# Two added waits in the start of a planned kernel: weight copies behind the first staging tile, and squares from the sixth token tile on

## The chip, the cores and the metric

The kernel runs on one core of a Trainium2 chip. Its metric is device time in microseconds (us) for one execution, as the median of several runs; lower is better. TensorE (PE) multiplies matrices, ScalarE (ACT), VectorE (DVE) and GpSimd (POOL) work element by element, and SyncE (SP) issues all of this kernel's DMAs from one queue, in program order. Each engine executes its own instructions in program order and waits on semaphores for the results of others.

## The reference, cut to what matters

One layer of a generator over 1024 latent tokens and 256 context tokens of width 1024, in float32. Both token sets are normalised, modulated and projected; two branches (gated linear attention and differential attention) follow, are merged and projected back. The change touches only the first two lines:

```python
def rms_norm(t):
    tf = t.astype(jnp.float32)
    return (tf * lax.rsqrt(jnp.mean(tf * tf, axis=-1, keepdims=True) + EPS)).astype(t.dtype)

mod_x = jax.nn.silu(c) @ w_ada[layer] + b_ada[layer]       # shift, scale, gate: 3 x 1024
mod_c = jax.nn.silu(c_ctx) @ w_ada[layer] + b_ada[layer]
h  = rms_norm(x) * (1 + sc_x) + sh_x                        # (1024, 1024)
hc = rms_norm(ctx) * (1 + sc_c) + sh_c                      # (256, 1024)
pl, pc = h @ w_in, hc @ w_in                                # eleven projections, 9248 columns
...
x = x + g_x * (y @ w_out)                                   # after both branches
```

## The kernel before, in words

**How the order comes about.** The program is written by a planner (`Driver`). Every piece of work is a Python generator that yields times, events or buffers; the planner keeps a clock of its own with a cost for each instruction, wakes the generators in the order of due time and priority (a lower number goes first), and the instructions are emitted in the order in which the generators run. The order on PE, ACT, DVE, POOL and in SP's queue is thus fixed when the program is built. An event such as `ev_h[k, half]` is set at the planned end of the work that it stands for; a generator that yields it resumes from then on. `acq(tag)` takes one of the buffers of a tag and waits until one is free. A few pieces have planned dates: the low-rank preparation 60 us, the output gate 70 us, late constants 105 us.

**Precision.** A float32 operand of a large product is split into a high part (fp32r) and a low part (the difference); a product is three matrix products (`mm3`, all emitted at line 349, high x high, high x low, low x high). Weights are split by an ACT copy for the high part and a DVE subtraction for the low part (`split`).

**The start of the program** (`prologue`, line 505, and `wstream`, line 686):

- *Token tiles.* Ten tiles of 128 tokens: 0 to 7 are latent, 8 and 9 context. `xnorm(i)` (line 515) takes a scratch buffer `p`, squares the tile on ACT with a sum (1024 elements per partition), forms the inverse root on POOL (two small instructions) and scales the tile on DVE. Tiles 0 to 3 are loaded early, between pieces of `w_ada`; tiles 4 to 9 after the modulation weights have been converted. Six tile buffers (`g5`) exist.
- *Modulation.* `w_ada` comes in two halves of the channels. The first half is used in float32 from tag `w` (`ada(0)`); the second is staged in tags `l5` and `raw` in turn, by 128 rows (row blocks 0 to 7), and split into tags `w` (even row blocks) and `pl` (odd ones; it holds the pieces of just one row block) by `conv` (line 566, priority -2), then multiplied on PE into `gs` and `go` (`ada(1)`). Each half ends in a small tile of shifts and scales, `shsc`.
- *Modulated channel blocks.* For each half of the latent tokens and then the context, and for each channel block k of 128 channels, PE transposes the normalised tiles into one of two `tp` buffers (line 375), and `hblock(k, half)` (line 640) modulates them on ACT (`p<-tp,shsc`), rounds the high part on POOL (`h<-p`) and subtracts on DVE (`h<-p,h`). Then `ev_h[k, half]` is set. Blocks 0 to 3 need the first half of `shsc`, blocks 4 to 7 the second. After block 7 the tile buffers of that half come free.
- *Projection weights.* `wstream` loads `w_in` into `raw` staging tiles of 256 rows (two blocks of 128), three buffers shared with the odd row blocks of `w_ada`, and splits them into tag `w` (18 buffers) with priority 3. The first stream has gates: its first two staging tiles are loaded behind the first half of `w_ada` (`RAWS = 2`), the others behind the second half; the splitting of the third and later ones waits until `conv` has ended. The split of the first two waits only for their data. A staging buffer comes free when both of its blocks have been split.
- *The first projection job.* `job_tr` (line 806) multiplies block by block: a first group of three outputs of 128 x 512, row blocks 0 to 7 with nine matrix products each (72), for the first half of the tokens, then a fourth group (24 products), then the context and the second half. It has priority 9, `ada` -1.

After the start, PE works through the projections, then both branches and the output.

The few lines around the change, in `wstream.run`:

```python
            for x, (n, src, c0, kk) in enumerate(queue):
                yield loaded[x]
                if gate and x == self.RAWS:
                    yield gate[2]
```

Of the kernel before, what the change touches and what calls it, by code (L numbers as in the profile page):

```python
# [232 lines left out]
class Hybrid:  # L233
# [271 lines left out]
    def prologue(self):  # L505
# [7 lines left out]
            self.dma(xs[i], a["x"][0, i * P:(i + 1) * P] if i < 8 else a["ctx"][0, (i - 8) * P:(i - 7) * P])  # L513

        def xnorm(i):
            yield from self.acq("p")
            sq = self.t("p", [P, D], BF16)
            ss = self.t("sm", [P, 1])
            yield self.d.when(xs[i])
            self.rel("p", self.act.activation(sq, xs[i], AF.Square, accum_out=ss))  # L520
            yield self.d.when(ss)
            self.pool.tensor_scalar(ss, ss, 1.0 / D, EPS, ALU.mult, ALU.add)
            yield self.pool.tensor_tensor(ss, ss, self.nhalf[:, 0:1], ALU.pow)
            self.d.set(ev_x[i], self.dve.tensor_scalar(xs[i], xs[i], ss, None, ALU.mult))
# [7 lines left out]
        def loads():  # L532

            for part in range(2):
                for k in range(NK):
                    src = wada[k * P:(k + 1) * P, 0:2048].rearrange("p (s h c) -> p s h c", h=2, c=512)[:, :, part]
                    ev = ev_w[k, part]
                    if part == 0:
                        yield from self.acq("w", 2)
                        ev.w = [self.t("w", [P, 512]) for _ in range(2)]  # L540
                        for s in range(2):
                            self.dma(ev.w[s], src[:, s])
                        d.set(ev, d.when(*ev.w))
                    else:
                        tg = ("l5", "raw")[k % 2]
                        yield from self.acq(tg)
                        raw = self.t(tg, [P, 2, 512])
                        self.dma(raw, src)
                        ev_r[k].raw = tg, raw
                        d.set(ev_r[k], d.when(raw))  # L550
                    for i in self.XL[part].get(k, ()):
                        yield from self.acq("g5")
                        xload(i)
                        self.d.spawn(xnorm(i))
                if part == 0:
                    d.set(self.ev_wl[0])
                    for x in range(self.RAWS):
                        yield self.wload[x]
            d.set(self.ev_wl[1])
            yield self.ev_wc  # L560
            for i in range(4, 10):
                yield from self.acq("g5")
                xload(i)
                self.d.spawn(xnorm(i))
# [121 lines left out]
    def wstream(self, jobs, tag, gate=None, prio=3, after=()):  # L686

        queue = [(n, src, c0, kk) for n, (src, c0) in enumerate(jobs) for kk in range(NK // 2)]
        wd = Weights({(n, k): Event() for n in range(len(jobs)) for k in range(NK)})
        loaded = [Event() for _ in queue]  # L690

        def load():
            for ev in after[:1]:
                yield ev
            for x, (n, src, c0, kk) in enumerate(queue):
                if gate and x in (0, self.RAWS):
                    yield gate[x > 0]
                yield from self.acq("raw")
                raw = self.t("raw", [P, 2, 512])
                loaded[x].raw = raw  # L700
                self.d.set(loaded[x], self.dma(raw, src[kk * 256:(kk + 1) * 256, c0:c0 + 512].rearrange(
                    "(k p) c -> p k c", p=P)))

        def run():
            for ev in after[1:]:
                yield ev
            for x, (n, src, c0, kk) in enumerate(queue):
                yield loaded[x]
                if gate and x == self.RAWS:
                    yield gate[2]  # L710
                raw = loaded[x].raw
                for j in range(2):
                    yield from self.acq(tag, 2)
                    hi = self.t(tag, [P, 512], F32R)
                    lo = self.t(tag, [P, 512], F32R)
                    e = yield from self.split(raw[:, j], hi, lo)
                    ev = wd[n, 2 * kk + j]
                    ev.w = (hi, lo)
                    self.d.set(ev, e)
                self.rel("raw", e)  # L720

        self.d.spawn(load(), prio=prio)
        self.d.spawn(run(), prio=prio)
        wd.loaded = loaded
        return wd
# [2080 lines left out]
```

## Time and profile before

| What | Value |
|---|---|
| median of 3 runs | 1617.54 us (1617.53 to 1622.0) |
| profiled execution, own time | 1616.59 us |
| its span | 1614.9 us, 24351 instructions |
| PE busy | 1590.6 us, 98% of the span |
| PE busy in the first 60 us | 48.67 us |
| DVE, ACT, POOL busy | 76%, 52%, 39% |
| HBM | 204 GB/s over the span |
| granted TensorE clock | 1.00 |

The times in the rows of the trace are from the span's start: the start, then the duration, the engine, the line, the operation, the output and inputs by tile names, the shapes, and the number of merged instructions; in brackets how long the engine stood idle before it and what ended that. Line 201 is the helper through which all ACT, DVE and POOL instructions go, 314 all DMAs, so one goes by tile names: `w<-raw` is a split of projection weights, `w<-l` and `pl<-raw` splits of modulation weights, `p<-g` the square of a token tile, `g<-g,sm` its scaling. Durations of PE rows are modelled and overlap, so the pace is read from starts.

### The profile page before, as it was taken

Reading aid. Unit: us, or ns where it says so; the run is one execution under the profiler, and the core shown is the slowest. Engines: PE = TensorE matmul, PEld = TensorE weight load, DVE = VectorE, ACT = ScalarE, POOL = GpSimd, SP = SyncE. Lnnn points to the kernel's source line nnn. Section 1 sums busy time; section 2 is a strip of 40 time slices with the busy share of each in tenths; the row PEclk is TensorE's granted clock in tenths of the full one; section 3 lists DMA queues with packets and bytes.
Section 4 is the critical chain, followed back from the end, with each engine's and each line's share of the span. In section 5 each row is a group of like instructions: output and inputs, shape, how many; then the busy total and the mean of one; then the engine's idle time right before and its main releaser. Section 6 shows DMA issues by size and latency. Waiting matters only on the chain.

```text
span 1614.9 us, 24351 instructions
## 1 busy us (share of the span) xinstructions
PE 1590.6 (98%) x8229; PEld 1328.0 (82%) x8229; DVE 1223.5 (76%) x2117; ACT 836.2 (52%) x1719; POOL 634.2 (39%) x663
## 2 busy tenths in 40 slices
PE   7999999999999999999999999999999999999999
PEld 3788888888888888888888788888888888888887
DVE  4787945576877779767677688878788888889994
ACT  4776523445343454655435466665665656656331
POOL 1500000001325667535464256656765666560000
PEclk9999999999999999999999999999999999999999
DMA  8576896998778467564645944545587555348662
GB/s 310 199 256 242 330 305 230 343 328 297 275 246 267 123 198 233 163 212 122 185 118 165 251 116 121 151 128 150 151 265 218 158 136 151 112 152 280 210 206 100
DMA packets 259565, 331.16 MB, mean 205 GB/s; under 512 B 22600, under 2 KB 160752, under 8 KB 259440
## 3 DMA queue, kind: packets, MB, share of 16 engines
q1 hardware_dynamic: 259440, 329.60, 63.7%
q8 instruction: 65, 1.06, 0.3%
q14 instruction: 60, 0.49, 0.1%
HBM read 225.20 MB, written 104.33 MB: 204 GB/s over the span
## 4 chain that ended last, share of the span: by engine, by line
PE 91%; DVE 4%; ACT 1%; DMA 1%; POOL 1%; issue 1%; SPq 0%; ACTq 0%; DVEq 0%; POOLq 0%
PE mm L349 31%; PE mb L349 11%; PE s L349 8%; PE mc L349 7%; PE b L349 6%; PE tp L349 6%; PE gt L349 5%; PE b L375 4%; PE gs L349 4%; PE go L349 4%; PE mz L349 2%; PE tp L375 2%; DVE sm L201 1%; POOL at L201 1%; DMA w<-in_w_ada 1%
## 5 line engine op out<-in xcount | busy, mean ns | idle before, releaser
L349 PE MATMUL mm<-w,h 128*128 128x512 f32 x912 | 231.0, 400 | 0.0
L349 PE MATMUL mb<-h,wt 128*128 128x512 f32 x840 | 222.8, 400 | 0.0
L201 DVE TENSOR_REDUCE sm<-s 128x1 f32<-128x1024 f32 (+1 forms) x192 | 193.3, 1037 | 16.4 <-PE s L349 9.9
L201 ACT ACTIVATE e<-s,sm 128x1280 f32<-128x1280 f32 x128 | 169.3, 1328 | 57.7 <-DVE sm L201 54.5
L349 PEld LDWEIGHTS mm<-w,h 128*128 128x128 f32 x912 | 167.4, 188 | 32.7
L201 POOL TENSOR_TENSOR at<-ac,at 128x512 fp32r<-128x512 f32 x128 | 186.6, 1458 | 10.7
L349 PEld LDWEIGHTS mb<-h,wt 128*128 128x128 f32 x840 | 151.4, 188 | 28.7 <-DVE ft L201 0.3
L201 POOL TENSOR_SCALAR at<-ac 128x512 fp32r<-128x512 f32 x128 | 98.4, 768 | 192.2 <-ACT ac L201 191.7
L349 PE MATMUL s<-hk,aq 128*128 128x512 f32 x744 | 169.2, 364 | 1.9 <-ACT e L201 1.8
L349 PE MATMUL mm<-h,w 128*128 128x512 f32 x672 | 168.2, 400 | 1.1 <-DVE h L201 1.1
L349 PEld LDWEIGHTS mm<-h,w 128*128 128x128 f32 x672 | 123.7, 188 | 26.5 <-DVE h L201 1.6
L201 DVE TENSOR_TENSOR w<-raw,w 128x512 fp32r<-128x512 f32 x128 | 95.7, 764 | 53.4 <-ACT w L201 51.2
L349 PEld LDWEIGHTS s<-hk,aq 128*128 128x128 f32 x744 | 117.6, 189 | 19.1 <-ACT e L201 4.3
L349 PE MATMUL b<-at,vv 128*128 128x256 f32 x960 | 130.1, 287 | 1.1 <-ACT ac L201 0.8
L349 PEld LDWEIGHTS b<-at,vv 128*128 128x128 f32 x960 | 119.5, 191 | 2.8 <-ACT ac L201 1.0
L201 ACT ACTIVATE w<-raw 128x512 fp32r<-128x512 f32 x128 | 78.1, 626 | 84.0 <-PE tp L349 23.8
L201 DVE SCALAR_TENSOR_TENSOR e<-e,sm,e 128x1280 f32<-128x1280 f32 x64 | 118.3, 1849 | 0.9
L201 ACT ACTIVATE ac<-b 128x512 f32<-128x512 f32 x122 | 72.4, 598 | 88.8 <-PE b L375 87.1
L201 POOL TENSOR_TENSOR sm<-sm,nhalf 128x2 f32<-128x2 f32 (+2 forms) x94 | 107.2, 1141 | 28.1 <-DVE sm L201 22.8
L349 PE MATMUL mm<-w,g 128*128 128x512 f32 x432 | 105.7, 389 | 0.0
L349 PEld LDWEIGHTS mm<-w,g 128*128 128x128 f32 x432 | 81.1, 188 | 16.8
L375 PE MATMUL b<-ident,e 128*128 128x128 f32 x610 | 92.6, 273 | 1.3 <-ACT ac L201 0.8
(353 smaller groups left out, 3050.8 us busy)
## 6 DMA issues: line engine op xcount, KB each, us to landing
raw<-in_w_in SPq DMA_DIRECT2D x62, 512.0 KB, 4.2
g<-d_s SPq DMA_DIRECT2D x32, 640.0 KB, 6.3
g<-d_s SPq DMA_DIRECT2D x32, 512.0 KB, 5.8
aq<-d_qT SPq DMA_DIRECT2D x124, 128.0 KB, 3.3
d_dv<-pl SPq DMA_DIRECT2D x40, 256.0 KB, 3.3
gv<-d_v SPq DMA_DIRECT2D x40, 256.0 KB, 3.2
d_kT<-pl SPq DMA_DIRECT2D x40, 256.0 KB, 2.7
hk<-d_kT SPq DMA_DIRECT2D x32, 320.0 KB, 5.7
```

The lines of the kernel that those rows point to most:

```text
L201: self.ins = f(out, *args, **kw).ins
L349: self.ins = self.nc.tensor.matmul(out, lhsT, rhs, start=start, stop=stop, skip_group_check=more).ins
L375: self.nc.tensor.transpose(out, src, self.ident[:n, :n])
```

## The change

Two waits are added. A normalisation `xnorm(i)` of tile 5 and later does not take its scratch buffer, and so does not square its tile, before channel block 5 of the first half of the tokens has been finished (`ev_h[5, 0]`). And in the first weight stream, which alone has gates, the split of the second staging tile (x == 1, projection rows 256 to 511) does not begin before channel block 1 of the first half has been finished (`ev_h[1, 0]`). No instruction is added or removed; loads are written by the same generators as before.

```diff
         def xnorm(i):
+            if i >= 5:
+                yield self.ev_h[5, 0]
             yield from self.acq("p")
             sq = self.t("p", [P, D], BF16)
             ss = self.t("sm", [P, 1])
...
                 yield loaded[x]
                 if gate and x == self.RAWS:
                     yield gate[2]
+                if gate and x == 1:
+                    yield self.ev_h[1, 0]
                 raw = loaded[x].raw
                 for j in range(2):
                     yield from self.acq(tag, 2)
```

## The prediction

> **What bounds the kernel now.** I read the page first (engines, slices), then busy time by stage, then the instructions in order of time on each engine between 22 and 62 us.
>
> ```profile
> span 1614.9 us, 24351 instructions
> PE 1590.6 (98%) x8229; PEld 1328.0 (82%) x8229; DVE 1223.5 (76%) x2117; ACT 836.2 (52%) x1719; POOL 634.2 (39%) x663
> ```
>
> ```profile
> 24.00:28.00 4.00, 2.89 (x22) 2.22 (x22) 3.30 (x8) 3.66 (x7) 1.40 (x2) 1.00 1.05 379
> 28.00:32.00 4.00, 4.00 (x19) 3.20 (x19) 3.59 (x5) 3.85 (x8) 1.98 (x3) 1.00 0.88 328
> 32.00:36.00 4.00, 4.00 (x17) 1.35 (x16) 4.00 (x8) 2.29 (x4) 0.00 (x0) 1.00 0.59 187
> ...
> 44.00:50.60 6.60, 3.82 (x28) 2.59 (x26) 5.34 (x11) 6.52 (x12) 4.02 (x7) 1.00 0.88 273
> 60.00:500.00 440.00, 438.68 (x2004) 363.55 (x2003) 308.41 (x462) 211.01 (x344) 57.97 (x55) 1.00 0.78 274
> 500.00:900.00 400.00, 398.48 (x2003) 335.34 (x2002) 293.28 (x551) 192.78 (x514) 216.37 (x269) 1.00 0.60 178
> 900.00:1614.90 714.90, 704.80 (x4031) 604.90 (x4030) 588.97 (x1050) 397.29 (x801) 343.17 (x304) 1.00 0.56 169
> ```
>
> The columns of a stage are its length, then busy time of PE, PEld, DVE, ACT and POOL, the granted clock, DMA share and GB/s. After 60 us PE is idle for only 1.32 + 1.52 + 10.10 = 12.9 us in 1555 us, so PE work sets the end there, and the granted clock is 1.00 in every stage shown. The change can act where PE is not yet fed: 24 to 28 us (1.11 us idle) and 44 to 50.6 us (2.78 us idle). Both holes are the same event: PE has transposed the first token tiles and waits until the channel blocks have been modulated (ACT), rounded to the high part (POOL) and given their low part (DVE).
>
> **Holding back the second staging tile.** The first hole, engine by engine:
>
> ```profile
> 24.65 1.15 ACT L201 ACTIVATE w<-raw 128x512 fp32r<-128x512 f32 x2 [0.21 <-DMA raw<-in_w_in]
> 25.71 3.02 ACT L201 ACTIVATE p<-tp,shsc 128x512 f32<-128x512 f32 x4
> ```
>
> ```profile
> 24.41 1.09 PE L375 MATMUL tp<-ident,g 128*128 128x128 f32 x8
> ...
> 27.60 4.50 PE L349 MATMUL mm<-h,w 128*128 128x512 f32 x18
> ...
> 35.25 2.92 PE L349 MATMUL mm<-h,w 128*128 128x512 f32 x12
> 38.01 0.63 PE L349 MATMUL gs<-pl,cs 128*2 128x512 f32 x2
> ```
>
> ```profile
> 24.72 1.89 DVE L201 TENSOR_TENSOR w<-raw,w 128x512 fp32r<-128x512 f32 x3
> 27.21 0.69 DVE L201 TENSOR_TENSOR h<-p,h 128x512 fp32r<-128x512 f32 x1 [0.60 <-POOL h L201]
> 28.41 2.11 DVE L201 TENSOR_TENSOR h<-p,h 128x512 fp32r<-128x512 f32 x2 [0.51 <-POOL h L201]
> ...
> 34.66 1.28 DVE L201 TENSOR_TENSOR pl<-raw,pl 128x512 fp32r<-128x512 f32 x2
> ```
>
> The ACT pair at 24.65 is what the new wait moves. It ends at 25.80 and the first modulation follows it directly. Its own input is there earlier: four of the eight transposes of 1.09 us are done at about 24.95. With about 0.1 us of handover (an estimate, the size of the small gaps between these rows) it could start at 25.05. *Gain: 25.71 - 25.05 = 0.66 us*, and the chain behind it (POOL, DVE, the 18 products at 27.60) moves along.
>
> What is moved comes back: two ACT copies (1.15 us) and two DVE subtractions (two thirds of 1.89, 1.26 us), now behind channel block 1's subtraction, which ends at 29.46 here and at 28.8 then. There ACT is busy for 3.85 of 4 us and DVE for 3.59 and 4.00 of 4, so on those engines nothing hides them: what follows on DVE, the pieces of the second half of the modulation weights, comes up to 1.26 - 0.66 = 0.60 us later than now. On PE it is hidden. PE has 18 products (4.50 us) before it needs block 2 of the projection weights, and the third pair of modulation pieces (DVE 34.66 + 1.28 = 35.94) is not used on PE before 38.01: 2.07 us of cover. I take 0. The bounds are +0.60, and -2.07 if PE's written order now takes that piece as soon as it is there.
>
> The third thing is a buffer. There are three staging buffers, and the load behind the second tile goes through the one SP queue:
>
> ```profile
> 26.64 0.37 SPq L314 DMA_DIRECT2D raw<-in_w_ada  x1
> ```
>
> ```profile
> raw<-in_w_ada SPq DMA_DIRECT2D x4, 512.0 KB, 5.9
> ```
>
> ```profile
> 38.44 1.15 ACT L201 ACTIVATE pl<-raw 128x512 fp32r<-128x512 f32 x2 [2.75 <-PE gs L349]
> ```
>
> The load at 26.64 (modulation row block 5) leaves when the second tile's subtractions end. They would end at 28.8 + 0.6 (first copy) + 1.3 (two subtractions) = 30.7 at the earliest, and 2.5 us later, 33.2, if row blocks 0 and 1 are copied first (four subtractions). With 5.9 us to land, block 5 is there at 36.6 to 39.1. It is copied at 38.44 now, which is 37.8 after the gain. I take 0; the upper bound is 39.1 - 37.8 = 1.3 us. What stands behind it in SP's order is held with it.
>
> **Holding back the squares.** The second hole:
>
> ```profile
> 46.01 1.04 ACT L201 ACTIVATE p<-g 128x1024 bf16<-128x1024 f32 x1
> 46.96 0.19 ACT L201 ACTIVATION_READ_ACCUMULATOR p<-g 128x1 f32 x1
> 47.05 1.43 ACT L201 ACTIVATE p<-tp,shsc 128x512 f32<-128x512 f32 x2
> ```
>
> ```profile
> 46.20 0.17 DVE L201 TENSOR_TENSOR shsc<-shsc,gt 128x16 f32<-128x16 f32 x1
> ...
> 48.36 1.10 DVE L201 TENSOR_SCALAR g<-g,sm 128x1024 f32<-128x1024 f32 x1 [0.72 <-POOL sm L201]
> 49.39 1.08 DVE L201 TENSOR_TENSOR h<-p,h 128x512 fp32r<-128x512 f32 x1
> ```
>
> ```profile
> 47.77 0.56 POOL L201 TENSOR_TENSOR sm<-sm,nhalf 128x1 f32<-128x1 f32 x1
> 48.30 3.67 POOL L201 TENSOR_SCALAR h<-p 128x512 fp32r<-128x512 f32 x4
> ```
>
> ```profile
> 50.53 8.25 PE L349 MATMUL mm<-h,w 128*128 128x512 f32 x35 [1.05 <-DVE h L201]
> 58.62 1.03 PE L375 MATMUL tp<-ident,g 128*128 128x128 f32 x8
> ```
>
> Tile 5 is in the way of channel block 4 three times. On ACT its square delays the modulation from about 46.45 (shift and scale end at 46.37) to 47.05: 0.60 us. On POOL its power ends at 48.33, and block 4's rounding starts at 48.30 instead of about 47.3 (the modulation would end near 47.2): 1.0 us. On DVE its scaling ends at 49.46, and block 4's subtraction starts at 49.39; without both it would start where the rounding ends, 47.3 + 0.92 + 0.15 = 48.4 (0.92 is a quarter of 3.67, 0.15 an estimated handover): again 1.0 us. PE waits for that subtraction at 50.53. These are one path, so *the gain is 1.0 us*, not the sum. Lower bound 0.45, if a weight copy of 0.58 us (half of 1.15) takes the slot on ACT: the modulation then still starts near 47.05, but POOL takes it up at its end, near 47.85, instead of at 48.30; upper bound 1.4, if the subtraction, no longer entangled with the scaling, takes 0.69 instead of 1.08.
>
> The 1.08 us stands beside a busy POOL; the same shape takes 0.69 at 27.21. [...]
>
> Where does tile 5 go? Behind block 5's subtraction, into these gaps:
>
> ```profile
> 53.07 1.06 ACT L201 ACTIVATE p<-g 128x1024 bf16<-128x1024 f32 x1 [2.21 <-DMA g<-in_x]
> ```
>
> ```profile
> 54.31 0.19 POOL L201 TENSOR_SCALAR sm<-sm 128x1 f32<-128x1 f32 x1 [2.34 <-ACT p L201]
> ```
>
> ```profile
> 55.16 0.75 DVE L201 TENSOR_SCALAR g<-g,sm 128x1024 f32<-128x1024 f32 x1 [0.85 <-POOL sm L201]
> 56.64 0.75 DVE L201 TENSOR_SCALAR g<-g,sm 128x1024 f32<-128x1024 f32 x1 [0.72 <-POOL sm L201]
> ```
>
> ACT has 2.21 us for the square and the read of its sum (1.04 + 0.19), POOL 2.34 for 0.19 + 0.56, DVE 0.85 for 0.75: cost 0. Tiles 6 to 9 get the same wait, but their data lands only at 53.07, after block 5's subtraction (about 52.5). If the gaps were gone, tile 7's scaling (end 57.39) would come up to 1.23 us later, just at its use on PE at 58.62, which itself moves to 57.0; bounds 0 to +1.6 (57.39 + 1.23 - 57.0).
>
> **After the holes.** A gain in front is kept only if PE has other work until the second half of the tokens is modulated. One job has a fixed date: the low-rank preparation starts at a planned 60 us.
>
> ```profile
> 59.41 3.66 PE L349 MATMUL mm<-h,w 128*128 128x512 f32 x15
> ...
> 63.26 1.63 PE L349 MATMUL mm<-h,pl 128*128 128x512 f32 x6
> ```
>
> The fourth group has 24 products, 15 of them here, so 9 x 0.24 us (3.66 / 15) = 2.2 us are left to fill in front of the low-rank work. That covers 1.66 us.
>
> **Sum.** -0.66 + 0 + 0 - 1.0 + 0 = -1.66 us. The profiled execution took 1616.59 us (its span and 1.69 us around it), so 1614.9 us for that one; it stands 0.95 us below the median of the runs, and against the median of 1617.54 the sum gives 1615.9 us. About 0.3%, 4.85 us, is what a measurement can tell from no change; the sum is a third of it.
>
> **The rivals.**
>
> *The held copies come too late* (slower). Place: row block 5 of the modulation weights, behind the second staging buffer on SP. For it: in 28 to 36 us ACT and DVE are full, and the planner gives the modulation copies priority over the projection copies. If row blocks 0 to 2 go first, the second tile is done at 34.66 (where the third pair starts) - 0.66 + 1.26 = 35.3, block 5 lands at 41.2 instead of being copied at 37.8, and the chain behind it is 3.4 us late: -1.66 + 3.4 = +1.8, or 1619.3 us. The point from which it decides: release at 37.8 - 5.9 = 31.9 starts to cost, and from 33.6 on the whole is slower than before. Against it: the wait opens at 28.8, about when the four modulations end on ACT and the copies of row block 0 can start (25.71 + 3.02 = 28.73 now).
>
> *The modulation chain closes up* (faster). PE now writes 12 products (35.25) ahead of the third pair, which is ready 2.07 us earlier. With block 2's weights later the planner may put the pair first: -1.66 - 2.07 = -3.7, or 1613.8 us. Against it: the products then have to fill later gaps.
>
> *Hidden anyway.* The freed ACT slots go to weight copies (0.58 us each): the first gain is eaten by the 0.60 us on DVE, of the second 0.45 us is left. That is about -0.4 us, between 0 and -0.9, or 1617.1 us.
>
> *The rest is written anew.* The order on every engine comes from a planner whose clock starts earlier, while 60, 70 and 105 us stay fixed dates. The 12.9 us of PE idle after 60 us could shrink or grow by a third to a half, 4 to 6 us: about 1611 or 1623 us. For it: the stretch from 900 us, where 10.1 of the 12.9 us lie. Against it: the dates bear on work of the first 120 us, and from 60 to 500 us PE is idle for only 1.32 us.
>
> **How the numbers follow.** Chances: my forecast (a gain of 0.9 to 2.7 us) 0.38; hidden anyway 0.17; held copies late 0.13; chain closes up 0.10; order written anew, faster 0.10 and slower 0.12. The first four lie within 0.3%: 0.78; faster 0.10, slower 0.12. The likeliest case's own range is 1614.8 to 1616.7 us. The range takes the first four (1613.8 to 1619.3, with their bounds about 1613 to 1621) and about half of either tail of the last: 1611.5 to 1622.0.
>
> **What would show it.** First modulation (ACT, now 25.71) at about 25.05 with the copy pair behind the four modulations; block 4's subtraction on DVE near 48.4 - 0.7 = 47.7, and PE's long run of products, now from 50.53, from about 48.9; no scaling of tile 5 before it, its square near 50 to 52; the transposes at 58.62 near 57.0. Wrong would be: the load of row block 5 leaving after 32 us; its copy waiting for the DMA rather than for PE; DVE idle in front of tile 7's scaling; or PE idle after 60 us other than 12.9 us, by 2 us or more, which would mean that the later order moved and not the start.

## The result and the profile after

The changed kernel takes 1621.18 us (median; 1618.52 to 1624.29), the kernel before in the same series 1618.73 us (1617.08 to 1622.26). The ratio is 1.0014, with an interval of 1.0008 to 1.0021: **slower by about 2.4 us**. That is less than the 0.3% which the prediction counted as no change, and inside its range. But the interval excludes the forecast gain of 1.66 us (0.999).

Two cautions on single profiles. The profiled execution of before (1616.59 us) lies below all 19 executions timed here. That of after (1623.29 us) is the second longest of its kernel's 19. A second profile of after (1621.22 us) sits at its median, and the accounting below uses that one. The profiled executions also begin up to 1.0 us apart, so milestones are counted from the first copy of projection weights on ACT (23.30 us in before, 24.03 in after, 23.54 in the second profile of after, 24.30 with the squares alone held and the constants late).

The page of after, and its busy time by stage (length, then busy time of PE, PEld, DVE, ACT and POOL, the granted clock, DMA share and GB/s):

```profile
span 1621.5 us, 24358 instructions
PE 1593.9 (98%) x8229; PEld 1329.0 (82%) x8229; DVE 1224.5 (76%) x2117; ACT 836.3 (52%) x1719; POOL 633.9 (39%) x663
```

```profile
40.00:44.00 4.00, 2.70 (x12) 0.88 (x10) 2.00 (x4) 2.66 (x6) 0.00 (x0) 1.00 0.76 295
44.00:50.60 6.60, 5.35 (x30) 2.93 (x31) 5.55 (x12) 5.73 (x11) 1.84 (x4) 0.92 0.91 310
50.60:60.00 9.40, 9.40 (x40) 7.84 (x40) 5.98 (x8) 6.17 (x10) 4.42 (x9) 0.88 1.00 346
60.00:500.00 440.00, 435.40 (x1987) 359.42 (x1986) 304.68 (x457) 211.45 (x347) 57.48 (x57) 1.00 0.77 271
```

Two stages are new against before: PE is idle for 1.30 us between 40 and 44 us, and for 4.60 us instead of 1.32 between 60 and 500 us. The clock below 1.00 is treated at the end.

ACT of after in order of time:

```profile
24.03 1.15 ACT L201 ACTIVATE w<-raw 128x512 fp32r<-128x512 f32 x2 [0.37 <-DMA raw<-in_w_in]
25.89 3.04 ACT L201 ACTIVATE p<-tp,shsc 128x512 f32<-128x512 f32 x4 [0.71 <-PE tp L375]
...
29.86 0.62 ACT L201 ACTIVATE w<-raw 128x512 fp32r<-128x512 f32 x1
...
31.43 0.62 ACT L201 ACTIVATE w<-raw 128x512 fp32r<-128x512 f32 x1
...
41.34 1.15 ACT L201 ACTIVATE pl<-raw 128x512 fp32r<-128x512 f32 x2 [4.60 <-DMA raw<-in_w_ada]
...
69.44 0.78 ACT L201 ACTIVATE p<-tp,shsc 128x512 f32<-128x512 f32 x1 [3.44 <-DMA d_k<-p]
```

The first row is the first staging tile; the first modulation follows it without the second tile between. The two held copies come at 29.86 and 31.43, one by one, between copies of modulation weights. Then two waits for a DMA: 4.60 us for row block 5 of the modulation weights, and 3.44 us for a *store* (`d_k<-p`). The store matters because it holds a scratch buffer `p` that the next modulation needs.

DVE and SP of after show why row block 5 is late:

```profile
33.06 0.68 DVE L201 TENSOR_TENSOR w<-raw,w 128x512 fp32r<-128x512 f32 x1
33.66 0.68 DVE L201 TENSOR_TENSOR pl<-raw,pl 128x512 fp32r<-128x512 f32 x1
34.26 0.68 DVE L201 TENSOR_TENSOR w<-raw,w 128x512 fp32r<-128x512 f32 x1
```

```profile
32.56 0.37 SPq L314 DMA_DIRECT2D l<-in_w_ada  x1
34.37 0.97 SPq L314 DMA_DIRECT2D raw<-in_w_ada  x2
...
50.82 0.82 SPq L314 DMA_DIRECT2D g<-in_x  x2
...
55.18 3.07 SPq L314 DMA_DIRECT2D gains<-in_diff_q_norm  x1
...
62.12 3.09 SPq L314 DMA_DIRECT2D d_k<-p  x3
```

The held tile's second subtraction ends at 34.94, and only then is its staging buffer free. With it held, the loads of row blocks 5 and 7 leave SP as a pair, one at 34.37 and one at 34.97, behind the load of row block 6 (32.56). The first of the pair is row block 5. By the times it takes the buffer of row block 1, whose second subtraction (33.66) ends at 34.34; the held tile's own buffer goes to row block 7. In before, row block 5 took the second staging tile's buffer and left at 26.64; row block 7 left at 33.55. The later rows show the second new thing. The loads of constants (`gains` and three like it) stand right ahead of the stores, and SP is held 3.07 us at the first of them. In before three of the four stood ahead of the token tiles and only `gdif` behind them, and three stores took 1.32 us to issue:

```profile
45.29 0.46 SPq L314 DMA_DIRECT2D gains<-in_diff_q_norm  x1
...
48.89 0.81 SPq L314 DMA_DIRECT2D g<-in_x  x2
...
52.46 1.83 SPq L314 DMA_DIRECT2D gdif<-in_diff_norm  x1
...
58.56 1.32 SPq L314 DMA_DIRECT2D d_k<-p  x3
```

From issue to landing the same three stores take 3.1 us in before and 7.3 in after (5.6 in its second profile):

```profile
d_k<-p SPq DMA_DIRECT2D x3, 256.0 KB, 3.1
```

```profile
d_k<-p SPq DMA_DIRECT2D x3, 256.0 KB, 7.3
```

While the stores stand behind the constants, little moves. In the second profile of after, where SP issues them from 60.92 on and they land after 68 us, the DMA share (the last figure but one) is 0.19 and 0.22 before it rises again:

```profile
60.00:62.00 2.00, 1.39 (x8) 0.97 (x6) 1.05 (x2) 2.00 (x7) 1.28 (x3) 1.00 0.19 52
62.00:64.00 2.00, 2.00 (x10) 1.64 (x9) 1.00 (x4) 2.00 (x9) 0.00 (x0) 1.00 0.22 80
64.00:66.00 2.00, 2.00 (x13) 1.58 (x12) 1.55 (x2) 0.80 (x2) 1.75 (x2) 1.00 0.88 321
```

PE of after shows what each costs:

```profile
42.75 0.62 PE L349 MATMUL gs<-pl,cs 128*2 128x512 f32 x2 [1.30 <-DVE pl L201]
...
51.08 9.30 PE L349 MATMUL mm<-h,w 128*128 128x512 f32 x36
...
60.98 0.77 PE L375 MATMUL tp<-ident,g 128*128 128x128 f32 x5 [0.26 <-DVE g L201]
62.15 3.71 PE L349 MATMUL mm<-h,w 128*128 128x512 f32 x15 [0.41 <-ACT p L201]
...
70.27 0.66 PE L375 MATMUL tp<-ident,g 128*128 128x128 f32 x4 [2.16 <-ACT p L201]
```

**Milestones in us behind the first weight copy.** Each is read from the start of a row on ACT or PE, less that of the copy; "last modulation product" is the last product of the second half of `w_ada`, "first use of block 4's low part" the 38th projection product. The long wait of PE behind the stores (70.27 above) stands before later transposes of the second half than the milestone, which is the first of them. The second profile of before took 1619.20 us.

| | before | before, 2nd profile | after, 2nd profile | squares only, constants late | both, row block 5 elsewhere, constants late |
|---|---|---|---|---|---|
| first modulation (ACT) | 2.41 | 2.40 | 1.86 | 2.41 | 1.87 |
| last modulation product | 20.62 | 21.18 | 21.90 | 20.61 | 19.95 |
| first use of block 4's low part | 27.23 | 28.60 | 27.28 | 26.22 | 26.22 |
| second half's first transposes | 35.32 | 37.45 | 35.36 | 34.31 | 34.66 |
| seventh low-rank product | 42.22 | 44.36 | 46.30 | 41.97 | 41.18 |
| first product `mm<-hk,w` | 55.39 | 57.53 | 59.48 | 55.14 | 58.43 |
| end | 1591.56 | 1593.70 | 1595.85 | 1592.60 | 1598.88 |

In the second profile of after, up to the second half's first transposes everything cancels against the first profile of before (+0.04 us): row block 5 costs 1.28, and block 4 gives 1.23 back. Between there and the seventh low-rank product 4.04 us are lost, and behind 75 us little more: +4.09 at the first product `mm<-hk,w`, +4.29 at the end.

The medians differ by only 2.4 us, and the second profile of before shows a reason. It has lost 2.13 us by the second half's first transposes, and nothing behind them. Its clock was at half for 3.41 us twice (the last section), and one weight copy waited for its data just ahead of block 4:

```profile
47.47 0.63 ACT L201 ACTIVATE w<-raw 128x512 fp32r<-128x512 f32 x1 [1.05 <-DMA raw<-in_w_in]
```

Against that profile after loses 2.15 us (1595.85 - 1593.70). The runs' mean granted clocks say the same. Of 86 executions of before in the experiments' series, 22 have a mean clock of 1.000, with a median of 1617.69 us. Of the 30 executions of after on record it is 15, with a median of 1621.18. Without loss of clock the change thus costs about 3.5 us. The medians of all executions show less, since before lost clock in more of its executions; why it did is not shown.

### The profile page after: what moved, and what is told of

The parts are those of the page before. It is cut to its first block, busy times and chain, and to the rows that moved or that the text cites. A ratio compares the mean times of both kernels' runs of the same rounds, so it can differ in the third digit from the quotient of the medians.

```text
span 1621.5 us, 24358 instructions
## 1 busy us (share of the span) xinstructions
PE 1593.9 (98%) x8229; PEld 1329.0 (82%) x8229; DVE 1224.5 (76%) x2117; ACT 836.3 (52%) x1719; POOL 633.9 (39%) x663
## 4 chain that ended last, share of the span: by engine, by line
PE 89%; DVE 4%; DMA 3%; ACT 1%; issue 1%; POOL 1%; SPq 0%; ACTq 0%; DVEq 0%; POOLq 0%
PE mm L349 29%; PE mb L349 11%; PE s L349 8%; PE mc L349 7%; PE b L349 6%; PE tp L349 6%; PE gt L349 5%; PE b L375 4%; PE go L349 4%; PE gs L349 4%; PE mz L349 2%; PE tp L375 2%; DVE sm L201 1%; POOL at L201 1%; DVE e L201 1%
```

## The experiments

These theories were at stake, with the numbers that the expectations give them. **Late row block** (1): the held copies keep a staging buffer, and row block 5 comes late. **Late tiles** (2): the waiting squares make the second half of the tokens late. **Constants in SP's order** (3): loads of constants have moved to right ahead of stores that hold scratch buffers. **Squares** (4): holding the squares gains at block 4 and loses it behind. Ratios are to the kernel before in the same series, whose medians were 1619.48 us (the first four runs below), 1618.74 (the next four) and 1618.99 (the last three).

**One wait at a time, and after once more.** The copies' wait alone:

```diff
+                if gate and x == 1:
+                    yield self.ev_h[1, 0]
```

> Only the wait of the second staging tile's copies is kept. Theory 1 (the held copies release their staging buffer late, the load of modulation row block 5 leaves late, and the modulation chain with it): slower by 2 to 3 us, about 1621 us beside 1618.7 us for the kernel before; the copy of row block 5 on ACT waits for its DMA and starts 2.5 to 3 us later than before, and PE stands idle in front of it for over 1 us. Theory 2 (the waiting squares make the second half of the tokens late): no loss here, 0.3 to 0.7 us faster, because the first modulation starts earlier.

Measured: 1.0019 (1.0010 to 1.0027), 1622.02 us. The late row block is there: its copy on ACT waits for the DMA (40.81), and the modulation chain ends 1.14 us later than in before (21.76). PE stands idle for it only 0.22 us, and not over 1 us as expected, since a pause of the clock (0.83 from 24 to 28 us, 0.74 from 28 to 32) had made PE late already. The wait behind the stores is there too (2.27 us before the second half's transposes at 68.96). By tile names (each engine's instructions in order, trace against trace), the order on ACT and DVE differs from before's only up to 34 us, by the two copies and two subtractions that are held; in SP's queue it differs up to 52 us.

The squares' wait alone:

```diff
+            if i >= 5:
+                yield self.ev_h[5, 0]
```

> Only the wait of the squares from tile 5 on is kept. Theory 1: faster by about 1.0 us, 1617.7 us, as channel block 4's subtraction no longer stands behind tile 5; no PE idle of more than 0.5 us between 58 and 75 us. Theory 2: slower by about 2.5 us, 1621 us, with PE idle of 2 us or more between 58 and 75 us, before the transposes of the second half.

Measured: 1.0006 (0.9998 to 1.0015), 1620.48 us. No row block is late, but the stores are (6.8 us to landing). ACT and PE of this kernel:

```profile
47.53 0.63 ACT L201 ACTIVATE w<-raw 128x512 fp32r<-128x512 f32 x1 [1.13 <-DMA raw<-in_w_in]
...
67.39 2.97 ACT L201 ACTIVATE p<-tp,shsc 128x512 f32<-128x512 f32 x4 [3.70 <-DMA d_k<-p]
```

```profile
68.22 1.32 PE L375 MATMUL tp<-ident,g 128*128 128x128 f32 x8 [2.15 <-ACT p L201]
```

ACT's freed slot was taken by a weight copy that waits for its own data (47.53): the gain at block 4 is 0.34 us here. The second profile of before has the same wait without the change (47.47 above), so it can be chance of an execution. The wait behind the stores does not need the held copies: either wait brings it.

> The changed kernel itself, for a second trace. Theory 1: PE idle of over 1 us in front of row block 5 (near 41 to 43 us) comes again, as the order on SP and ACT is the same. Open: the stall of 2.2 us before the second half's transposes near 70 us and the lower granted clock between 44 and 60 us; if they are chance of one execution they are absent here, if they follow from the late start they come again. Time: 1621.2 us, 2.4 us above the kernel before.

Measured: 1.0019 (1.0010 to 1.0028), 1621.22 us, with 2.46 us of idle PE at the same transposes and 1.28 us on the modulation chain. The loss of clock between 44 and 60 us did not come again (1.00), the other two did.

**Row block 5 in another buffer.** Both waits; row block 5 goes to a free tile of tag `x4` instead of the held staging buffer:

```diff
-                        tg = ("l5", "raw")[k % 2]
+                        tg = "x4" if k == 5 else ("l5", "raw")[k % 2]
```

> Both waits are kept, but modulation row block 5 is staged in another buffer (tag x4, which is empty until the output gate's date of 70 us) and so no longer waits for the held copies. Theory 1: the loss is gone, and the gain that was forecast comes out: 1.7 us faster than the kernel before, 1617.0 us; the copy of row block 5 waits for PE and not for its DMA. Theory 2: still slower than before by 1 to 2.5 us, with the PE idle between 58 and 75 us unchanged.

Measured: 1.0040 (1.0027 to 1.0052), 1625.93 us, slower than after. Locally it does what it should: the modulation chain ends at 20.88, 0.26 behind before instead of 1.28. But the planner writes another order, and the 1617.0 us expected are missed by 9: PE waits for ACT at 62.76, and between 150 and 200 us it is busy 47.83 of 50 us, where it is busy all of the time in before:

```profile
62.76 0.96 PE L349 MATMUL mm<-h,w 128*128 128x512 f32 x3 [3.00 <-ACT p L201]
```

```profile
100.00:150.00 50.00, 49.92 (x220) 40.66 (x219) 38.58 (x58) 36.31 (x51) 0.62 (x1) 1.00 0.81 285
150.00:200.00 50.00, 47.83 (x204) 38.46 (x203) 44.02 (x72) 28.73 (x44) 0.00 (x0) 0.97 0.79 288
```

So the local price of the late row block is shown, the worth of its repair for the whole is not.

**Constants out of the stores' way.** Three tiles of constants are cleared on POOL ahead of their loads (three small instructions). The loads then leave behind the stores, at 78 to 84 us instead of 45 to 59. By tile names nothing else moves on ACT, DVE and POOL, and in SP's queue only the load of `rope` in some of the kernels. This was done to both waits, to each alone, and to the kernel before, which itself was run once more as it is.

```diff
         self.gains = g = self.c("gains", [P, 2, 2, 64])
+        self.pool.memset(g, 0.0)
...
         self.ggla = self.c("ggla", [P, 256])
+        self.pool.memset(self.ggla, 0.0)
...
         self.gdif = self.c("gdif", [P, P])
+        self.pool.memset(self.gdif, 0.0)
```

> The kernel before, for a second trace, as its first one (1616.6 us) lies below its median (1619.5 us in the last comparison). Theory 3: the stall of 2.2 to 2.6 us that the trace of every variant shows before the transposes of the second half (near 68 us) comes from SP's order: the loads of the gains stand behind the loads of tiles 6 to 9 there and in front of them here, and the first three stores, which hold scratch buffers that ACT needs, land 3 us later. By theory 3 the stall is absent here too (under 0.5 us of PE idle between 58 and 75 us, stores landing in about 3 us). Rival: the stall is chance of an execution and comes here as well. Time ratio 1.000.

Measured: 1.0002 (0.9993 to 1.0011), 1619.2 us. The wait is absent: the three stores land in 2.4 us, and PE has no idle time at the transposes (67.35 and 69.61).

```profile
d_k<-p SPq DMA_DIRECT2D x3, 256.0 KB, 2.4
```

> The kernel before with the hold on the three constant tiles alone. Theory 3: nothing changes in the start, as the stall is absent either way: within 0.7 us of the kernel before. If the loads of the constants also cost the kernel before something (they stand in front of the loads of tiles 6 and 7), up to 1 us faster.

Measured: 1.0002 (0.9993 to 1.0011), 1618.86 us. Where the stores are not late, moving the constants is worth nothing.

> The changed kernel with one thing more: each of the three constant tiles (gains, the two norm gains) is first cleared on POOL at its planned date, so that its loads cannot be issued before and stand behind the first stores on SP. Theory 3: the stall before the second half's transposes goes (PE idle there under 0.8 us instead of 2.2 to 2.6 us), the stores land in 3 to 4 us instead of 7, and the kernel gains about 2.3 us on the changed one: 1619 us, as fast as the kernel before within 0.5 us; the late row block 5 (1.3 us) stays. Rival (the stall follows from the late tiles, not from SP's order): stall and time as in the changed kernel, 1621 to 1622 us.

Measured: 1.0008 (0.9999 to 1.0017), 1620.39 us, 1.4 us above the 1619 expected. The wait for the stores is gone. ACT waits for PE at the same point, and PE keeps only the wait for the scaling of tile 7:

```profile
68.16 0.78 ACT L201 ACTIVATE p<-tp,shsc 128x512 f32<-128x512 f32 x1 [1.93 <-PE tp L375]
```

```profile
61.25 0.76 PE L375 MATMUL tp<-ident,g 128*128 128x128 f32 x5 [1.14 <-DVE g L201]
62.39 5.30 PE L349 MATMUL mm<-h,w 128*128 128x512 f32 x15 [0.37 <-ACT p L201]
```

The 15 products at 62.39 take 5.30 us instead of 3.71, since the clock was at half from 62.55 to 65.96, so this execution lost 1.6 us at the same place by the clock. SP's being held is not by itself the harm: in this kernel it stands 4.57 us at another load (`rope`, 53.92), and no one waits for a store. In before it stood 1.83 us at `gdif`, in after 3.07 at `gains`, each time at the load right behind that of `p<-in_w_in`. What differs is what is queued right ahead of the stores.

> Only the wait of the squares, with the same hold on the three constant tiles. Theory 3: no stall, no late row block 5, so what is left is the gain of 0.3 to 1.2 us in front of channel block 4: 1618.5 us beside 1619.5 us for the kernel before. Rival: the stall stays, 1620.5 us or more.

Measured: 1.0001 (0.9992 to 1.0010), 1618.75 us: level with before. ACT and PE:

```profile
58.42 1.06 ACT L201 ACTIVATE p<-g 128x1024 bf16<-128x1024 f32 x1
...
59.47 1.55 ACT L201 ACTIVATE p<-mm 128x512 f32<-128x512 f32 x3
```

```profile
58.61 1.03 PE L375 MATMUL tp<-ident,g 128*128 128x128 f32 x8
60.10 3.72 PE L349 MATMUL mm<-h,w 128*128 128x512 f32 x15 [0.46 <-ACT p L201]
```

Here block 4 gives the 1.0 us of the prediction (26.22 against 27.23). Then 0.7 us of it go. The fourth group starts 1.49 us behind the transposes instead of 0.79 (59.41 - 58.62 in before), since the copies of the first group's results (`p<-mm`, 59.47) stand on ACT behind the squares of the context tiles; in before those had ended by then. What stays at the first product `mm<-hk,w` is 0.25 us, and behind it this execution loses 1.29 us more against before's first (end +1.04).

> Only the wait of the second staging tile's copies, with the hold on the three constant tiles, so that the stall before the second half cannot hide its own price. Theory: what is left is the late row block 5: last modulation product 1.1 to 1.3 us later against the first weight copy than in the kernel before, no stall of over 1 us near 68 us, and 1.0 to 1.5 us slower than the kernel before, 1620 us. Rival (the copies' wait costs nothing by itself, the stall was all): within 0.5 us of the kernel before.

Measured: 1.0010 (1.0001 to 1.0019), 1620.57 us, some 1.6 us: the price of the held copies alone, with the modulation chain 1.28 us late (21.90 against 20.62).

The three pairs with and without the moved constants are 1.0019 and 1.0008 (both waits), 1.0019 and 1.0010 (copies), 1.0006 and 1.0001 (squares). Each pair's intervals overlap. Together they point one way: a mean of 0.0008, 1.3 us, where the profiles show 2.2 to 2.5 us of idle PE gone. By the medians alone, each against its series' before, it is 0.0004. So it is shown that the constants' place makes the wait; what the wait costs in time is not settled. The profile of the copies' wait with constants late lost clock just ahead of this place (the last section), so only the squares show the gain without a pause: the first product `mm<-hk,w` comes 3.0 us earlier (55.14 against 58.16). Among executions with a mean clock of 1.000, the medians without and with the moved constants are 1621.2 and 1619.4 us (both waits), 1621.9 and 1619.4 (copies), 1619.8 and 1618.6 (squares), but the second ones come from 4, 1 and 7 executions.

**Holding the context tiles longer.** The squares' wait, constants late, and tiles 8 and 9 held for the second half's first block, so that the results' copies come first:

```diff
             if i >= 5:
                 yield self.ev_h[5, 0]
+            if i >= 8:
+                yield self.ev_h[0, 1]
```

> The wait of the squares with the hold, and the squares of the context tiles 8 and 9 wait for the first modulated block of the second half. Theory 4: with the squares alone the 1.0 us gained in front of block 4 was lost again at the fourth group's products near 60 us, because ACT copies the first group's results only behind the squares of tiles 8 and 9. By it these copies now start about 2.4 us earlier, PE does not wait for them, and the gain of 0.9 to 1.0 us reaches the first context products: 1617.7 us beside 1618.7 us. Rival: another wait of the second half takes its place and the time is that of the squares with the hold, 1618.7 us.

Measured: 1.0052 (1.0039 to 1.0064), 1627.16 us, the slowest of all, where either 1617.7 or 1618.7 was expected. The copies do come first (ACT 57.75, and no wait on PE at 60 us). But the rest is written anew, and PE waits at 121 to 124 and 168 to 172 us for weights:

```profile
100.00:150.00 50.00, 47.91 (x210) 38.65 (x210) 38.74 (x63) 34.61 (x49) 0.62 (x1) 1.00 0.81 290
150.00:200.00 50.00, 47.58 (x208) 38.51 (x207) 44.36 (x70) 29.69 (x45) 0.00 (x0) 1.00 0.80 290
```

**Row block 5 elsewhere and constants late.** Both edits on top of both waits:

> Both waits, row block 5 staged in the other buffer, and the hold. Theory: the modulation chain is as early as in the kernel before, within 0.3 us against the first weight copy. In SP's order the next weight loads (pl) now stand in front of the first three stores, so a part of the stall may come back; without it 1618 us, with it 1620 to 1622 us. By the theory of SP's order the stall's size follows the stores' landing: about 3 us landing, no stall; 6 us or more, 2 us of stall.

Measured: 1.0037 (1.0024 to 1.0050), 1624.02 us, above the 1618 to 1622 expected, though the stores land in 2.1 us. In front it is the best: the modulation chain ends 0.67 us ahead of before (19.95 against 20.62: the predicted first gain, 0.66, once no row block is late), block 4's use 1.01 us ahead, and the seventh low-rank product 1.04 us ahead. By the first product `mm<-hk,w` it is 3.04 us behind, and 4.15 us more are lost between there and the first attention score (824.95 us between the two, 820.80 in before). No version was faster than the kernel before. A sixth scratch buffer `p`, which would loosen the hold of the stores directly, was not tried.

## Why the prediction was wrong, point by point

- **The first modulation (-0.66): right, but not carried.** It starts 0.55 us earlier (2.41 to 1.86). The gain reaches the end of the modulation chain only where row block 5 is not late (the 0.67 above).
- **"The third thing is a buffer ... I take 0": a term of the sum that was mis-sized.** The buffer was named, and the value taken was the wrong one. The load was to leave at 30.7 to 33.2 and to land in 5.9 us. It left at 34.37, which is 33.6 on the clock of before (0.73 us less), and landed about 6.9 us later. It went into row block 1's buffer, because the held tile's came free later still (34.94): ACT put the two held copies between copies of row blocks, and DVE their subtractions between those of row block 1. Row block 5 was copied at 41.34 (40.6) instead of landing between 36.6 and 39.1, and the chain ended 1.28 us later instead of 0.66 earlier. This is the rival "the held copies come too late", whose landing time (41.2) was near. Its price was not: it had the chain 3.4 us late; PE had other products to put first, and the chain lost 1.28 + 0.66 = 1.9 us against the forecast. The copies' wait by itself, with the constants out of the way, measures some +1.6 us against before (0.2 to 3.1).
- **Block 4's subtraction (-1.0): right where it stands alone.** Squares held and constants late: 1.01 us. With the squares alone it was 0.34, by the mechanism of "hidden anyway", a weight copy in the freed slot on ACT. In after it is in balance with the late row block. The 0.15 us from rounding to subtraction were the author's estimate; at channel block 0 of before the subtraction (27.21) starts 0.04 us behind the end of its rounding (26.55 + 0.62). The upper bound of 1.4, with a subtraction of 0.69 us, did not come: with the squares held and constants late, where the scaling of tile 5 is not beside it, the subtraction still takes 1.09 us (49.38). Why it takes longer there than at 27.21 is not shown. In before it began 0.51 us after a rounding on POOL (48.88), and that rounding too takes longer than the one ahead of it (1.05 against 0.62 us); no run isolates it.
- **Tile 5 and those behind it "into these gaps: cost 0": wrong, within its bounds.** In the second profile of after the fourth group starts 2.05 us behind the transposes (60.95 - 58.90) instead of 0.79: 1.26 us lost, of a bound of 1.6. One part is the scaling of tile 7, as named (0.18 to 1.14 us of idle PE in the kernels with both waits). The other was not: the copies of the first group's results on ACT, behind the squares of the context tiles.
- **"After the holes": the step that failed outright.** It asked only whether PE had work until the second half of the tokens was modulated, and counted products. It didn't ask whether that modulation could get its scratch buffers. These are held by stores in SP's queue, and SP's order had changed: PE's idle time at the second half's transposes, 2.2 to 2.5 us, is the largest single loss in after's profiles. The prediction had quoted no row of SP behind 27 us. The sign that it named for such a case, PE idle time after 60 us other by 2 us or more, did show: 4.60 + 0.05 + 11.60 = 16.25 us instead of 12.9.
- **"The rest is written anew" (4 to 6 us): the order was, the price came in three experiments only.** By tile names, after's order differs from before's on ACT up to 377 us and on DVE up to 395. The copies' wait alone changes it only up to 34 us, so it is the squares' wait that rewrites the rest. Behind the first product `mm<-hk,w` this is worth +0.2 us in after's second profile and +0.8 in its first. The edits on `x4` and on the context tiles brought 3 to 8 us against what the same waits cost without them (ratios 1.0040 against 1.0019, 1.0037 against 1.0008, 1.0052 against 1.0001).

The 4.3 us are those of two executions without a pause of the clock, the 2.4 those of the medians. In after a pause was also hidden in part by the wait for the stores: in its first profile the second half's first transposes come 0.84 us later than in the second (36.20 against 35.36), the seventh low-rank product only 0.35 (46.65 against 46.30). Why SP's order put the constants behind the token tiles was not settled either; the runs show only that either wait is enough to bring it about.

## What to carry to other kernels

Where a wait holds back one consumer of a ring of buffers, follow the *buffer*, and the next buffer of the ring that a load can take in its place: add up, on every engine between the new start and the release, the work that has a higher priority, and take the late end of that sum rather than the middle. After a re-planning, the DMA queue's order is a term of the sum like any engine's: list which stores hold buffers that the next stage needs, and what is queued ahead of them. And a local fix in a kernel whose order is planned as a whole is priced by the whole: two edits here that repaired their place cost 3 us or more elsewhere, up to a hundred microseconds later.

## What the runs showed of the hardware that was not expected

In some of the profiled executions, of before and after alike, the granted clock of TensorE stood at 0.50 for some microseconds: in after from 49.48 to 52.89, in the second profile of before from 50.64 to 54.05. In both PE had just been idle in part, for 0.48 us up to 49.47 and for 1.91 us up to 49.86. The clock was 1.00 throughout in the profile that the prediction had, which therefore counted nothing for it. Stages of before in its second profile, and of the kernel with the copies' wait and constants late, and PE's long run of products in the latter:

```profile
50.60:60.00 9.40, 9.02 (x35) 7.18 (x36) 7.07 (x9) 6.41 (x11) 6.40 (x10) 0.82 0.92 313
```

```profile
50.60:60.00 9.40, 8.81 (x28) 6.60 (x27) 7.18 (x9) 6.34 (x12) 5.14 (x9) 0.64 1.03 384
```

```profile
52.54 10.81 PE L349 MATMUL mm<-h,w 128*128 128x512 f32 x35 [0.57 <-DVE h L201]
```

The 35 products take 10.81 us there, against 8.25 in before: 2.6 us. In after they are 36 in 9.30, where 8.25 / 35 x 36 = 8.49 would be the full pace: 0.8 us. The clock time lost in the two stages is 0.18 x 9.4 = 1.7 us and 0.36 x 9.4 = 3.4 us. Narrower stages show the pauses themselves, 3.41 us at 0.50 in the first kernel and 6.83 us at 0.50 in the second:

```profile
50.64:54.05 3.41, 3.03 (x9) 2.23 (x10) 3.41 (x4) 2.21 (x4) 3.06 (x4) 0.50 0.74 251
```

```profile
51.25:58.08 6.83, 6.26 (x16) 4.59 (x15) 5.33 (x8) 4.07 (x8) 3.15 (x5) 0.50 1.02 397
```

What starts and what ends such a pause is not shown. PE's idle time ahead of it does not tell by itself: in before 2.78 us of idle time lay between 44 and 50.6 us, in pieces, and in its second profile 2.68, and the stage behind came out at 1.00 in one execution and at 0.82 in the other. Two pauses stand in the start of the second profile of before (the other in 24 to 40 us, a stage at 0.89). Such pauses go with a good part of the 4 to 6 us by which executions of one kernel differ: before's executions with a mean clock of 1.000 have a median of 1617.69 us (22 of them), those with 0.998 one of 1619.60 (33), those with 0.996 one of 1621.63 (3). A single profile thus lay 2 us to either side of the median here: 1616.59 beside 1618.73 us in before, 1623.29 beside 1621.18 in after.
